# Four groups by seven products in each feed-forward stage, woven with ordinary steps, and silu as one ScalarE activation

## The chip, the cores and the metric

One core of a Trainium2 chip runs the whole kernel in one launch. The metric is the device time of one execution in microseconds (us). Engines are named as in the profile: PE is TensorE's matmul side and PEld its weight loads, DVE is VectorE, ACT is ScalarE, POOL is GpSimd, SP is SyncE, which issues nearly all loads.

## The reference, cut to what matters

The kernel computes one decoder block over 256 positions and a model width of 2048, in fp32:

```
h = x + 1/2 * SwiGLU_1(RMSNorm(h))          # feed-forward stage 1, inner width 5632 = 44 blocks of 128
h = h + W_out(mixer(RMSNorm(h) @ W_in))     # gated recurrence (8 heads) beside a short convolution
h = h + 1/2 * SwiGLU_2(RMSNorm(h))          # feed-forward stage 2, the same shape as stage 1
h = h + sigmoid(RMSNorm(h) @ W_pg) * (p @ W_pe)
y = RMSNorm_final(h)

swiglu(x) = (silu(x @ w_gate) * (x @ w_up)) @ w_down
```

The change touches the two feed-forward stages, the loop that emits all steps, and the sizes of some buffers that the mixer shares.

## The kernel before, in words

**Numbers in two parts.** Every fp32 weight block and every activation is split into a high part (a copy rounded to fp32r, made by ACT) and a low part (the rest, a subtraction by DVE). A product of two numbers is three matmuls: high by high, high by low, low by high. An ordinary step holds a 128-column block of weights (raw, 128 x 16 x 128 values): `load` (L100 ff.) issues its DMA on SP, `split` makes `hi` (L97, ACT) and `lo` (L98, DVE) in two halves of 128x1024, `product` (L116 ff.) runs for each of 16 k-blocks a 512-column matmul of `hi` (L120, both parts of the activation side by side) and a 256-column matmul of `lo` (L119 or L122). The epilogue adds the two halves of the PSUM bank (`halves`: ACT copy L146, DVE add L147) and scales it (L153).

**Feed-forward stage.** The inner width is cut into four chunks (`CHUNKS`: 8, 12, 12 and 12 blocks). For each chunk gate and up steps fill `hid`, then 16 down steps (each `nk` = 8 or 12 k-blocks) add into the residual `hT` (`partial`, L204 ff.: ACT L206, DVE L207 and L208). A gate epilogue is scaled, a Sigmoid (L158), and a DVE multiply (L375); an up epilogue multiplies with the gate (L381) and splits into `hid` (L162, L163).

**Groups by seven products.** In each of the last three chunks, four of the twelve blocks (4 gate and 4 up blocks together) are computed as a 2x2 block product with seven products in place of eight (Winograd's form): the tokens are two halves of 128, the k-blocks come in 8 pairs, and gate and up weights are 512 wide. `seven` (L273 ff.) makes 16 half steps out of a group: for each pair `kp` a half step "a" (3 products, 9 matmuls of 512 columns, lines L293 to L295) and a half step "b" (4 products, 12 matmuls). Seven PSUM banks of the eight hold the seven sums for the whole group, so one bank is left for the ordinary steps between. The combinations of the activations are made once per stage (`forms`, L253 ff.), written to DRAM by POOL's queue (L271) and read back with each pair (`xf`, L304). The weight combinations are made for each pair by DVE (`sp_a`, L320 to L322), and they are split like other weights (`pieces`, L309 ACT, L310 DVE). The group's raw weights have one buffer (`sraw`, `bufs=1`), loaded by L302. At the end `epi` (L335 ff.) adds the seven sums and applies silu (Sigmoid L343, two DVE multiplies L344, L345), and `turn` transposes the result into `hid` (L392, 8 transposes a group).

**Order.** The order is written out by hand. Each chunk with a group runs: two half steps, then ordinary gate or up step and half step in turn (14 of each), the last two ordinary steps, `turn`, then 16 down steps without any half steps. The main loop emits for step i: the load of step i + 3, the split of step i + 2, the matmuls of step i, its epilogue, its hooks. Hooks carry the extra work, such as `rows` at the stage's step 5 and `forms(kp)` at steps 6 + kp. From this the framework's scheduler makes one list of instructions per engine, which may differ from the order of the code where the inputs allow.

Of the kernel before, what the change touches and what calls it, by code (L numbers as in the profile page):

```python
# [14 lines left out]
P = 128  # L15
# [16 lines left out]

CHUNKS = ((8, 0), (12, 4), (12, 4), (12, 4))
NS = 4
NK2 = NB // 2

RAW_BUFS = 3
LOAD_AHEAD = 3
SPLIT_AHEAD = 2


class Step:


    def __init__(self, src, nk, mm, epi=None):
        self.src, self.nk, self.mm, self.epi = src, nk, mm, epi
        self.hooks = []
        self.before = self.after = self.ld = self.sp = None


@with_exitstack
def kernel(
# [87 lines left out]
    def new_ps():  # L140
        return psum.tile([P, T2], F32, tag="ps", name="ps")
# [84 lines left out]
    def add(*a, **k):  # L226
        steps.append(Step(*a, **k))
        return len(steps) - 1
# [12 lines left out]

    FA, FB = ("P1", "P2", "P6"), ("P5", "P3", "P7", "P4")
    FORMS = {"P4": 0, "P5": 1, "P6": 2, "P7": 3, "P3": 4}

# [8 lines left out]
    def forms(kp, c_gain, sd):  # L253
        pool = st["spool"]
        a = pool.tile([P, 5, P], F32, tag="ec", name="fa", bufs=2)
        f = pool.tile([P, 5, P], F32, tag="ey", name="ff", bufs=2)
# [5 lines left out]
        a11, a21, a12 = a[:, 0, :], a[:, 1, :], a[:, 2, :]  # L262
        V.tensor_tensor(a21, a21, rho, ALU.mult)
        V.tensor_tensor(f[:, 0, :], a[:, 3, :], rho, ALU.mult)
        V.tensor_tensor(f[:, 1, :], a21, f[:, 0, :], ALU.subtract)
        V.tensor_tensor(f[:, 2, :], f[:, 1, :], a11, ALU.subtract)
        V.tensor_tensor(f[:, 3, :], a11, a21, ALU.subtract)
        V.tensor_tensor(f[:, 4, :], a12, f[:, 2, :], ALU.add)
        A.activation(x[:, 0], f, AF.Copy)
        V.tensor_tensor(x[:, 1], f, x[:, 0].bitcast(F32), ALU.subtract)  # L270
        nc.gpsimd.dma_start(sd[:, kp, :], x.rearrange("p a f t -> p (a f t)").bitcast(F32))  # L271

    def seven(ws, sd, finish):  # L273
# [24 lines left out]
        def ld(kp):  # L298
            def f(s):
                pool = st["spool"]  # L300
                r = g["raw", kp] = pool.tile([P, 4, T2], F32, tag="sraw", name="sraw", bufs=1)
                nc.sync.dma_start(r, ws[kp])  # L302
                x = g["xf", kp] = pool.tile([P, 10 * P], F32, tag="xf", name="xf", bufs=2)
                nc.sync.dma_start(x, sd[:, kp, :])  # L304
            return f

        def pieces(hi, lo, todo):
            for sl, src in todo:
                A.activation(hi[:, sl, :], src, AF.Copy)  # L309
                V.tensor_tensor(lo[:, sl, :], src, hi[:, sl, :].bitcast(F32), ALU.subtract)  # L310

        def sp_a(kp):
            def f(s):
                pool, r = st["spool"], g["raw", kp]
                t = g["t", kp] = pool.tile([P, 3, T2], F32, tag="st", name="st", bufs=1)
                hi, lo = g["a", kp] = tuple(pool.tile([P, 3, T2], F32R, tag="a" + n, name="a" + n, bufs=1)
                                            for n in ("hi", "lo"))
                pieces(hi, lo, [(slice(0, 2), r[:, 0:2, :])])
# [3 lines left out]
                V.tensor_tensor(r[:, 3, :], t[:, 2, :], r[:, 1, :], ALU.add)  # L322
                pieces(hi, lo, [(2, t[:, 2, :])])
            return f

        def sp_b(kp):
            def f(s):
                pool, r, t = st["spool"], g["raw", kp], g["t", kp]
                hi, lo = g["b", kp] = tuple(pool.tile([P, 4, T2], F32R, tag="b" + n, name="b" + n, bufs=1)
                                            for n in ("hi", "lo"))  # L330

                pieces(hi, lo, [(slice(0, 3, 2), t[:, 0:2, :]), (slice(1, 4, 2), r[:, 2:4, :])])
            return f

        def epi(s):  # L335
            pool = st["spool"]

            def e(tag, bufs=2):
                return pool.tile([P, 5 * P], F32, tag=tag, name=tag, bufs=bufs)[:, :T2]
# [7 lines left out]
            a, c0, v = e("ea", 1), e("ec"), e("ey")  # L347
            A.activation(a, g["P1"], AF.Copy)
# [5 lines left out]
            V.tensor_tensor(a, g["P7"], a, ALU.add)  # L354
            c1 = e("ec")
            V.tensor_tensor(c1, g["P4"], a, ALU.add)
# [4 lines left out]
        for kp in range(NK2):  # L361
            for key, names, sp in (("a", FA, sp_a), ("b", FB, sp_b)):
                s = Step(None, 0, mm(kp, names, key), epi if key == "b" and kp == NK2 - 1 else None)
                s.sp = sp(kp)
                s.ld = ld(kp) if key == "a" else None
                res.append(s)
        return res

    def ffn(wg, wu, wsd, wd, c_gain, c_next, name):
# [15 lines left out]
        def turn(k0, c):  # L385

            for k in range(0, NS, 2):
                ps = new_ps()
                for i in range(2):
                    for w in range(2):  # L390
                        o = i * T + w * P
                        TE.transpose(ps[:, o:o + P], c[w][:, (k + i) * P:(k + i + 1) * P], ident)  # L392
                d = st["hid"][:, k0 + k:k0 + k + 2, :]
                p = ps.rearrange("p (k t) -> p k t", k=2)
                A.activation(d[:, :, :T], p, AF.Copy)
                V.tensor_tensor(d[:, :, T:], p, d[:, :, :T].bitcast(F32), ALU.subtract)

        i0 = len(steps)
        f0 = ng = 0
        for ci, (nf, ns) in enumerate(CHUNKS):  # L400
            last = ci == len(CHUNKS) - 1
            std = []
            for k in range(ns, nf):
                std.append(Step(wg[f0 + k], NB, *gemm_in(g_epi)))
                std.append(Step(wu[f0 + k], NB, *gemm_in(u_epi(k))))
            if ns:
                got = []
                h = seven(wsd[ng], sd, lambda *c, got=got: got.extend(c))
                ng += 1
                seq, std = [*h[:2]], std  # L410
                for x in h[2:]:
                    seq += [std.pop(0), x]
                seq += std
                seq[-1].hooks.append(lambda got=got: turn(0, got))
                steps.extend(seq)
            else:
                steps.extend(std)
            order = [*range(ns, nf), *range(ns)]
            for j in range(NB):
# [11 lines left out]
                add(wd[j][:, f0:f0 + nf, :], nf, mm, epi)  # L431
            f0 += nf
        at(i0 + 5, rows)
        for kp in range(NK2):
            at(i0 + 6 + kp, lambda kp=kp: forms(kp, c_gain, sd))

# [13 lines left out]
    def mixer():  # L450
# [590 lines left out]
```

## Time and profile before

| | us |
|---|---|
| median of 3 runs | 2029.08 (2026.64 to 2030.02) |
| the profiled execution, its own time | 2028.77 |
| its span, first to last instruction | 2027.0 |
| PE busy | 2002.1 (99%) |
| DVE busy | 1636.0 (81%) |
| ACT busy | 1117.1 (55%) |
| DMA, mean | 207 GB/s |

The span is what the trace covers; 1.8 us of the execution lie around it. Matmuls are pipelined, so a row's duration is longer than its share of PE: the distance from one start to the next is what a matmul costs. An engine that is off the critical path can be busy for 80% and still set when a buffer comes free.

### The profile page before, as it was taken

The numbers are of one execution on the slowest core, as the hardware profiler recorded it, in microseconds if no ns is written. First come the engines' busy times: TensorE is split into PE (matmuls) and PEld (weight loads), VectorE is DVE, ScalarE is ACT, GpSimd is POOL, SyncE is SP. The second block draws the span as 40 slices with busy tenths as digits, with TensorE's granted clock in tenths as the row PEclk, the third lists the DMA queues.
The fourth block names the chain that finished last, engine by engine and source line by source line (L and its number), as shares of the span: only waits on it lengthen the run. The fifth ranks groups of instructions, "written<-read, shape, count | busy, mean of one in ns | idle before, by whom it ended". The sixth has DMA issues, their size and how long they took to land.

```text
span 2027.0 us, 28859 instructions
## 1 busy us (share of the span) xinstructions
PE 2002.1 (99%) x11094; PEld 1731.7 (85%) x11094; DVE 1636.0 (81%) x2645; ACT 1117.1 (55%) x1716; POOL 11.6 (1%) x23
## 2 busy tenths in 40 slices
PE   8999999999999999999999999999999999999997
PEld 7888888888888888888888888888888888888886
DVE  8988886888688775689798789788968886887886
ACT  7655555555555554553566556455555555555663
POOL 0000000000000000000000000000000000000000
PEclk9999999999999999999999999999999999999998
DMA  8686666665665465544355567766666666654742
GB/s 293 211 277 242 233 205 216 219 237 200 222 232 198 156 212 187 189 166 146 129 184 187 187 227 274 226 232 226 208 208 224 232 202 220 228 202 153 249 164 84
DMA packets 69546, 419.93 MB, mean 207 GB/s; under 512 B 7712, under 2 KB 7968, under 8 KB 35744
## 3 DMA queue, kind: packets, MB, share of 16 engines
q1 hardware_dynamic: 67104, 407.60, 59.0%
q0 software_dynamic: 2304, 10.49, 1.3%
q8 instruction: 87, 1.43, 0.3%
q14 instruction: 51, 0.42, 0.1%
HBM read 405.48 MB, written 12.58 MB: 206 GB/s over the span
## 4 chain that ended last, share of the span: by engine, by line
PE 89%; DVE 4%; DMA 4%; issue 1%; ACT 1%; SPq 0%; DVEq 0%; ACTq 0%
PE ps L120 49%; PE ps L119 23%; PE ps L294 3%; PE ps L295 3%; PE ps L293 3%; PE ps L122 2%; DVE lo L98 2%; DMA sraw<-w1s 1%; DMA raw<-w1d 1%; DMA raw<-w1u 1%; PE ps L591 1%; PE ps L494 1%; PE ps L493 1%; PE ps L492 1%; DMA sraw<-w2s 1%
## 5 line engine op out<-in xcount | busy, mean ns | idle before, releaser
L120 PE MATMUL ps<-xs,hi 128*128 128x512 f32 x3056 | 1082.8, 395 | 9.5 <-DVE xs L167 6.1
L98 DVE TENSOR_TENSOR lo<-raw,hi 128x1024 fp32r<-128x1024 f32 (+2 forms) x660 | 751.1, 1139 | 239.3 <-ACT hi L97 235.7
L97 ACT ACTIVATE hi<-raw 128x1024 fp32r<-128x1024 f32 (+2 forms) x660 | 652.7, 990 | 516.6 <-PE ps L120 323.6
L119 PE MATMUL ps<-xs,lo 128*128 128x256 f32 x2865 | 801.5, 280 | 0.4 <-DVE lo L98 0.2
L120 PEld LDWEIGHTS ps<-xs,hi 128*128 128x128 f32 x3056 | 569.7, 188 | 137.5 <-ACT hi L97 7.2
L119 PEld LDWEIGHTS ps<-xs,lo 128*128 128x128 f32 x2865 | 538.0, 188 | 10.4 <-DVE lo L98 1.8
L120 PE MATMUL ps<-hid,hi 128*128 128x512 f32 x1384 | 477.6, 394 | 0.0
L119 PE MATMUL ps<-hid,lo 128*128 128x256 f32 x1258 | 354.4, 283 | 0.5 <-ACT hid L162 0.5
L120 PEld LDWEIGHTS ps<-hid,hi 128*128 128x128 f32 x1384 | 251.5, 188 | 48.8
L119 PEld LDWEIGHTS ps<-hid,lo 128*128 128x128 f32 x1258 | 236.2, 188 | 7.3 <-ACT hid L162 1.3
L309 ACT ACTIVATE ahi<-sraw 128x1024 fp32r<-128x1024 f32 x48 | 51.0, 1063 | 125.2 <-DMA sraw<-w1s 61.5
L146 ACT ACTIVATE t<-ps 128x256 f32<-128x256 f32 x191 | 70.2, 372 | 88.3 <-PE ps L120 88.3
L320 DVE TENSOR_TENSOR st<-sraw 128x1024 f32<-128x1024 f32 x48 | 58.8, 1224 | 69.2 <-DMA sraw<-w1s 38.7
L147 DVE TENSOR_TENSOR t<-ps,t 128x256 f32<-128x256 f32 x191 | 80.3, 421 | 24.0 <-ACT t L146 23.9
L120 PE MATMUL ps<-mixout,hi 128*128 128x512 f32 x240 | 83.6, 397 | 0.0
L153 DVE TENSOR_TENSOR t<-t,rb 128x256 f32<-128x256 f32 x183 | 76.9, 422 | 2.7
L293 PE MATMUL ps<-bhi,xf 128*128 128x512 f32 x192 | 74.9, 390 | 0.0
L295 PE MATMUL ps<-blo,xf 128*128 128x512 f32 x192 | 74.9, 390 | 0.0
L294 PE MATMUL ps<-bhi,xf 128*128 128x512 f32 x192 | 74.9, 390 | 0.0
L208 DVE SCALAR_TENSOR_TENSOR hT<-ps,t 128x256 f32<-128x256 f32 x141 | 59.7, 424 | 13.7 <-DVE t L207 1.4
L207 DVE TENSOR_TENSOR t<-hT,t 128x256 f32<-128x256 f32 x141 | 59.1, 420 | 10.6 <-ACT t L206 10.6
L206 ACT ACTIVATE t<-ps 128x256 f32<-128x256 f32 x141 | 51.9, 369 | 27.5 <-PE ps L120 27.5
(234 smaller groups left out, 2078.7 us busy)
## 6 DMA issues: line engine op xcount, KB each, us to landing
raw<-w_in SPq DMA_DIRECT2D x48, 1024.0 KB, 4.8
raw<-w1d SPq DMA_DIRECT2D x48, 768.0 KB, 4.2
raw<-w2d SPq DMA_DIRECT2D x48, 768.0 KB, 4.3
raw<-w2g SPq DMA_DIRECT2D x32, 1024.0 KB, 4.9
raw<-w2u SPq DMA_DIRECT2D x32, 1024.0 KB, 5.1
raw<-w1u SPq DMA_DIRECT2D x31, 1024.0 KB, 5.3
raw<-w1g SPq DMA_DIRECT2D x30, 1024.0 KB, 5.0
xf<-forms SPq DMA_DIRECT2D x48, 640.0 KB, 4.0
```

Of the source, the lines that this page charges most:

```text
L97: A.activation(hi[:, sl, :], r, AF.Copy)
L98: V.tensor_tensor(lo[:, sl, :], r, hi[:, sl, :].bitcast(F32), ALU.subtract)
L119: TE.matmul(ps[:, T:], lo, m[:, :T], start=False, stop=False)
L120: TE.matmul(ps, hi, m, start=first, stop=last)
L146: A.activation(t, ps[:, T:], AF.Copy)
L147: V.tensor_tensor(t, ps[:, :T], t, ALU.add)
L153: V.tensor_tensor(dst, t, rb, ALU.mult)
L207: V.tensor_tensor(t, hT[:, j, :], t, ALU.add)
L208: V.scalar_tensor_tensor(hT[:, j, :], ps[:, :T], c, t, ALU.mult, ALU.add)
L293: TE.matmul(g[p], x_lo, hi[:, i, :], start=kp == 0, stop=False)
L294: TE.matmul(g[p], x_hi, hi[:, i, :], start=False, stop=False)
L295: TE.matmul(g[p], x_hi, lo[:, i, :], start=False, stop=kp == NK2 - 1)
```

## The change

It does five things, in both feed-forward stages.

1. A fourth group replaces 4 more gate and 4 more up blocks. The chunks now have 0, 1, 1 and 2 groups.
2. `weave` spreads the half steps: group 1 among the gate and up steps of chunk 2, group 2 among the down steps of chunk 2, group 3 among the gate and up steps of chunk 3, group 4 among the down steps of chunk 3. `turn` becomes two steps of its own per group.
3. Silu is one ACT activation; the DVE multiplies L375 and L344 go.
4. The group's raw weights share the ring of raw buffers, now 4 deep (it was 3, and one for the groups). Loads are issued 4 steps ahead, splits up to 3 steps ahead with two rules that stop them. The combinations use one more form and one fewer special case, and the split of a half step's weights is one instruction per engine, 128x1536 or 128x2048.
5. `forms` runs at every second step, and some temporary buffers shrink (`t` 6 to 4, `s` 3 to 2, `nr` 4 to 3).

```diff
-CHUNKS = ((8, 0), (12, 4), (12, 4), (12, 4))
+CHUNKS = ((8, 0), (12, 1), (12, 1), (12, 2))
-RAW_BUFS = 3
-LOAD_AHEAD = 3
-SPLIT_AHEAD = 2
+RAW_BUFS = 4
+LOAD_AHEAD = 4
+SPLIT_AHEAD = 3
...
-    def tt(shape=(P, T), dtype=F32, tag="t", bufs=6):
+    def tt(shape=(P, T), dtype=F32, tag="t", bufs=4):
...
-        s = tt(tag="s", bufs=3)
+        s = tt(tag="s", bufs=2)
...
-        A.activation(x[:, 0], f, AF.Copy)
-        V.tensor_tensor(x[:, 1], f, x[:, 0].bitcast(F32), ALU.subtract)
+        A.activation(x[:, 0, 4, :], a22, AF.Copy)
+        A.activation(x[:, 0, :4, :], f, AF.Copy)
+        V.tensor_tensor(x[:, 1, 4, :], a22, x[:, 0, 4, :].bitcast(F32), ALU.subtract)
+        V.tensor_tensor(x[:, 1, :4, :], f, x[:, 0, :4, :].bitcast(F32), ALU.subtract)
...
-                r = g["raw", kp] = pool.tile([P, 4, T2], F32, tag="sraw", name="sraw", bufs=1)
+                r = wpool.tile([P, NB, P], F32, tag="raw", name="raw", bufs=RAW_BUFS)
+                r = g["raw", kp] = r.rearrange("p (a b) c -> p a (b c)", a=4)
...
+        def parts(key, kp, n, src):
+            hi, lo = g[key, kp] = tuple(st["spool"].tile([P, n, T2], F32R, tag=key + t, name=key + t, bufs=1)
+                                        for t in ("hi", "lo"))
+            A.activation(hi, src, AF.Copy)
+            V.tensor_tensor(lo, src, hi.bitcast(F32), ALU.subtract)
...
-                y = e("ey")
-                A.activation(y, c, AF.Sigmoid, scale=rt[:, 0:1])
-                V.scalar_tensor_tensor(c, c, rt[:, 0:1], y, ALU.mult, ALU.mult)
-                V.scalar_tensor_tensor(c, u, rt[:, 0:1], c, ALU.mult, ALU.mult)
+                y = e("ey", 2)
+                A.activation(y, c, AF.Silu, scale=rt[:, 0:1])
+                V.scalar_tensor_tensor(c, u, rt[:, 0:1], y, ALU.mult, ALU.mult)
...
+        (c0, d0), (c1, d1), (c2, d2), (c3, d3) = others
+        g1, g2, g3, g4 = groups
+        def alternate(x, h):
+            seq = [*h[:2]]
+            for i in range(2, 16):
+                seq += [x[i], h[i]]
+            return seq
+        steps.extend([*c0, *d0])
+        first = alternate([None, None, *c1[:14]], g1[0])
+        steps.extend([*first, *c1[14:], *g1[1]])
+        steps.extend([*d1[:2], *alternate(d1, g2[0])])
+        steps.extend([*c2[:2], *g2[1], *alternate(c2, g3[0])])
+        steps.extend([*d2[:2], *alternate(d2, g4[0])])
+        steps.extend([*c3[:2], *g3[1], *c3[2:4], *g4[1], *c3[4:], *d3])
...
-            s = sig(g)
-            V.tensor_tensor(g, g, s, ALU.mult)
+            A.activation(g, g, AF.Silu)
...
-            at(i0 + 6 + kp, lambda kp=kp: forms(kp, c_gain, sd))
+            at(i0 + 6 + 2 * kp, lambda kp=kp: forms(kp, c_gain, sd))
...
-            d = m["m1"].tile([P, T], F32R, tag="nr", name="nr", bufs=4)
+            d = m["m1"].tile([P, T], F32R, tag="nr", name="nr", bufs=3)
...
+    loaded = done = 4
     for i, s in enumerate(steps):
-        if 0 < i < n - LOAD_AHEAD:
-            load(steps[i + LOAD_AHEAD])
-        if 1 < i < n - SPLIT_AHEAD:
-            split(steps[i + SPLIT_AHEAD])
+        while i > 0 and loaded < min(n, i + LOAD_AHEAD + 1):
+            load(steps[loaded])
+            loaded += 1
+        while 1 < i and done < min(n, i + SPLIT_AHEAD + 1):
+            x = steps[done]
+            if x.kind == "w" and sum(y.kind == "w" for y in steps[i:done]) > 2:
+                break
+            if x.kind in ("a", "b") and any(y.kind == x.kind for y in steps[i:done]):
+                break
+            split(x)
+            done += 1
```

In `weave`, `c0` to `c3` are the gate and up steps of the chunks, `d0` to `d3` their down steps; `g[0]` is the 16 half steps of a group and `g[1]` its two `turn` steps.

## Rows read from the trace of the kernel before

**Rows 1.** The page: the span, and busy time of each engine.

```profile
span 2027.0 us, 28859 instructions
...
PE 2002.1 (99%) x11094; PEld 1731.7 (85%) x11094; DVE 1636.0 (81%) x2645; ACT 1117.1 (55%) x1716; POOL 11.6 (1%) x23
```

**Rows 2.** Timeline of PE, 199.5 to 218 us: start us, us, then the instruction.

```profile
199.80 0.40 PE L293 MATMUL ps<-bhi,xf 128*128 128x512 f32 x1
...
202.53 0.40 PE L120 MATMUL ps<-xs,hi 128*128 128x512 f32 x1
...
208.15 0.39 PE L293 MATMUL ps<-ahi,xs 128*128 128x512 f32 x1
...
210.23 0.40 PE L120 MATMUL ps<-xs,hi 128*128 128x512 f32 x1
```

**Rows 3.** Timeline of PE: first group's transposes, first down step, second group's start.

```profile
277.96 1.04 PE L392 MATMUL ps<-cst,ec 128*128 128x128 f32 x8
278.75 0.48 PE L120 MATMUL ps<-hid,hi 128*128 128x512 f32 x1
...
346.34 0.39 PE L293 MATMUL ps<-ahi,xs 128*128 128x512 f32 x1
```

**Rows 4.** Windows over six group stretches: length, engines' busy (count), PEclk, DMA share, GB/s.

```profile
148.98:278.75 129.77, 129.59 (x689) 110.44 (x688) 113.01 (x153) 73.68 (x100) 0.00 (x0) 1.00 0.66 227
346.34:476.65 130.31, 129.95 (x690) 110.37 (x688) 111.50 (x150) 73.38 (x99) 0.00 (x0) 1.00 0.65 226
544.24:673.58 129.34, 129.34 (x689) 110.45 (x688) 107.13 (x144) 70.14 (x95) 0.00 (x0) 1.00 0.60 209
1316.96:1446.15 129.19, 129.19 (x689) 110.63 (x688) 111.62 (x150) 73.93 (x99) 0.00 (x0) 1.00 0.64 224
1513.74:1644.39 130.65, 129.50 (x689) 110.55 (x688) 111.82 (x150) 73.68 (x99) 0.00 (x0) 1.00 0.64 225
1711.98:1841.51 129.53, 129.53 (x689) 110.47 (x688) 107.49 (x144) 70.37 (x95) 0.00 (x0) 1.00 0.59 209
```

**Rows 5.** Timelines of SP, DVE and PE around 1580 us; in brackets idle before.

```profile
1571.89 0.33 SPq L302 DMA_DIRECT2D sraw<-w2s  x1
...
1579.53 1.23 DVE L320 TENSOR_TENSOR st<-sraw 128x1024 f32<-128x1024 f32 x1 [4.08 <-DMA sraw<-w2s]
...
1584.06 0.51 PE L120 MATMUL ps<-xs,hi 128*128 128x512 f32 x1 [1.15 <-DVE t L147]
```

**Rows 6.** First chunk of stage 1: PE's two idle times, and the windows row.

```profile
60.03 0.50 PE L120 MATMUL ps<-xs,hi 128*128 128x512 f32 x1 [0.96 <-ACT hi L97]
...
70.13 0.39 PE L122 MATMUL ps<-xs,lo 128*128 128x256 f32 x1 [1.16 <-DVE lo L98]
...
45.00:103.00 58.00, 55.88 (x318) 48.10 (x317) 56.93 (x141) 39.12 (x69) 3.87 (x7) 1.00 0.60 207
```

**Rows 7.** Groups by line of DVE, shapes apart: busy, mean ns, idle before.

```profile
L98 DVE TENSOR_TENSOR lo<-raw,hi 128x1024 fp32r<-128x1024 f32 x460 | 562.2, 1223 | 144.6 <-ACT hi L97 141.4
L98 DVE TENSOR_TENSOR lo<-raw,hi 128x768 fp32r<-128x768 f32 x192 | 183.4, 957 | 93.9 <-ACT hi L97 93.5
...
L321 DVE TENSOR_TENSOR st<-st,sraw 128x512 f32<-128x512 f32 x48 | 32.9, 685 | 0.0
```

**Rows 8.** Timeline of DVE, three instructions with no idle time between them.

```profile
204.06 0.42 DVE L163 TENSOR_TENSOR hid<-t,hid 128x256 fp32r<-128x256 f32 x1
204.40 1.22 DVE L310 TENSOR_TENSOR blo<-st,bhi 128x1024 fp32r<-128x1024 f32 x1
205.53 1.22 DVE L310 TENSOR_TENSOR blo<-sraw,bhi 128x1024 fp32r<-128x1024 f32 x1
```

**Rows 9.** Groups by line: what frees a down step's PSUM bank.

```profile
L208 DVE SCALAR_TENSOR_TENSOR hT<-ps,t 128x256 f32<-128x256 f32 x141 | 59.7, 424 | 13.7 <-DVE t L207 1.4
...
L206 ACT ACTIVATE t<-ps 128x256 f32<-128x256 f32 x141 | 51.9, 369 | 27.5 <-PE ps L120 27.5
```

**Rows 10.** Timeline of ACT: the table load ahead of the first Sigmoid.

```profile
51.88 1.28 ACT L158 ACT_TABLE_LOAD   x1
```

More of the change, by code (lines that the diff above doesn't have):

```diff
@@ L48, in __init__ @@
         self.before = self.after = self.ld = self.sp = None
+        self.kind = "w"
 @with_exitstack
@@ L312, in sp_a @@
         def sp_a(kp):
             def f(s):
[L314 to L318, printed above, removed]
+                r = g["raw", kp]
+                parts("a", kp, 3, r[:, 0:3, :])
@@ L326, in sp_b, with e @@
         def sp_b(kp):
[L327 to L333, printed above, removed]
+            return lambda s: parts("b", kp, 4, g["t", kp])
         def epi(s):
             pool = st["spool"]
-            def e(tag, bufs=2):
-                return pool.tile([P, 5 * P], F32, tag=tag, name=tag, bufs=bufs)[:, :T2]
+            def e(tag, bufs):
+                return pool.tile([P, T2], F32, tag=tag, name=tag, bufs=bufs)
@@ L348, in epi @@
+            a, c0, v = e("ea", 1), e("ec", 4), e("ey", 2)
             A.activation(a, g["P1"], AF.Copy)
@@ L364, in seven @@
                 s.sp = sp(kp)
+                s.kind = key
                 s.ld = ld(kp) if key == "a" else None
@@ L367, in seven, with weave @@
         return res
+    def weave(groups, others):
+        (c0, d0), (c1, d1), (c2, d2), (c3, d3) = others
[12 more added lines that the diff above has]
+        steps.extend([*c3[:2], *g3[1], *c3[2:4], *g4[1], *c3[4:], *d3])
     def ffn(wg, wu, wsd, wd, c_gain, c_next, name):
@@ L385, in turn, with step, mm, epi @@
         def turn(k0, c):
[L387 to L396, printed above, removed]
+            def step(k):
+                def mm(s):
+                    s.ps = new_ps()
+                    for i in range(2):
+                        for w in range(2):
+                            o = i * T + w * P
+                            TE.transpose(s.ps[:, o:o + P], c[w][:, (k + i) * P:(k + i + 1) * P], ident)
+                def epi(s):
+                    d = st["hid"][:, k0 + k:k0 + k + 2, :]
+                    p = s.ps.rearrange("p (k t) -> p k t", k=2)
+                    A.activation(d[:, :, :T], p, AF.Copy)
+                    V.tensor_tensor(d[:, :, T:], p, d[:, :, :T].bitcast(F32), ALU.subtract)
+                s = Step(None, 0, mm, epi)
+                s.sp = lambda s: None
+                s.kind = None
+                return s
@@ L398, in ffn @@
+            return [step(k) for k in range(0, NS, 2)]
         i0 = len(steps)
-        f0 = ng = 0
-        for ci, (nf, ns) in enumerate(CHUNKS):
+        groups = []
+        others = []
+        f0 = 0
+        for ci, (nf, ng) in enumerate(CHUNKS):
             last = ci == len(CHUNKS) - 1
-            std = []
-            for k in range(ns, nf):
+            for i in range(ng):
+                got = []
+                h = seven(wsd[len(groups)], sd, lambda *c, got=got: got.extend(c))
+                groups.append((h, turn(i * NS, got)))
+            std, down = [], []
+            for k in range(ng * NS, nf):
@@ L404, in ffn @@
                 std.append(Step(wg[f0 + k], NB, *gemm_in(g_epi)))
                 std.append(Step(wu[f0 + k], NB, *gemm_in(u_epi(k))))
[L406 to L417, printed above, removed]
@@ L418, in ffn @@
-            order = [*range(ns, nf), *range(ns)]
+            order = [*range(ng * NS, nf), *range(ng * NS)]
             for j in range(NB):
@@ L430, in epi @@
                         partial(s.ps, j, 0.5)
-                add(wd[j][:, f0:f0 + nf, :], nf, mm, epi)
+                down.append(Step(wd[j][:, f0:f0 + nf, :], nf, mm, epi))
+            others.append((std, down))
             f0 += nf
+        weave(groups, others)
         at(i0 + 5, rows)
         for kp in range(NK2):
-            at(i0 + 6 + kp, lambda kp=kp: forms(kp, c_gain, sd))
+            at(i0 + 6 + 2 * kp, lambda kp=kp: forms(kp, c_gain, sd))
         def open_hid(s):
@@ L1007, in sevens @@
         res, f0 = [], 0
-        for nf, ns in CHUNKS:
-            if ns:
-                g, u = (w[:, f0 * P:(f0 + NS) * P].reshape(NK2, 2, P, NS * P) for w in (gate, up))
+        for nf, ng in CHUNKS:
+            for i in range(ng):
+                c = slice((f0 + i * NS) * P, (f0 + (i + 1) * NS) * P)
+                g, u = (w[:, c].reshape(NK2, 2, P, NS * P) for w in (gate, up))
                 res.append(np.stack([g[:, 0], g[:, 1], u[:, 1], u[:, 0]], 2))
```

35 lines of the change are left out of this document (14 added, 21 removed).

## Prediction

> **What bounds the kernel now.** I read the page first. PE is busy for 2002.1 of 2027.0 us, DVE for 81% of the span [rows 1]. So PE is the bound, and only two things can make the kernel faster: fewer matmul columns, or less of the 25 us in which PE idles. The execution took 2028.77 us, 0.31 below the median of 2029.08; I apply the sum to the median.
>
> PE's timeline gives the price of each kind of step as a distance between starts. In a group stretch a half step b lasts 202.53 - 199.80 = 2.73 us, an ordinary gate or up step 208.15 - 202.53 = 5.62, a half step a 210.23 - 208.15 = 2.08 [rows 2]. The 8 transposes of a group take 278.75 - 277.96 = 0.79, and 16 down steps of 12 blocks (346.34 - 278.75) / 16 = 4.22 each [rows 3].
>
> The six stretches from a group's first half step to the end of its transposes hold 16 ordinary steps, 8 a, 8 b and the transposes: 16 x 5.62 + 8 x (2.08 + 2.73) + 0.79 = 129.19 us with no wait at all. They took 129.19 to 130.65, 3.65 us more in sum [rows 4]. So PE hardly waits there, though DVE is busy for 83 to 87% of them. The largest wait shows the mechanism: the group's raw weights have one buffer, their load was issued at 1571.89, DVE stood 4.08 us until it landed at 1579.5, and the bank of the ordinary step before was then emptied late, so PE idled 1.15 us at 1584.06 [rows 5]. PE also idles 0.96 and 1.16 us in the first chunk of stage 1, where DVE is busy for 56.93 of 58 us [rows 6]. There `forms` runs at eight steps in a row.
>
> **The change, part by part.**
>
> *A fourth group.* It takes 8 ordinary steps away, 8 x 5.62 = 44.96 us, and adds 8 x (2.08 + 2.73) + 0.79 = 39.27 [rows 2, 3]. That is 5.69 less per stage, 11.4 for both, all of it on PE and so on the path. A 512-column matmul costs (208.15 - 202.53) x 2/3 / 16 = 0.234 us here by its share of columns, at a granted clock of 1.00, that is 2.4 GHz [rows 2, 4]. The Trainium skill (TensorE: Matmul & The Clock Gate, section "Wait — 56ns, not 53.3ns?") gives start to start the columns over 2.4 GHz plus about 2.5 ns, which is 0.216. The trace does not agree, and the measurement decides; by the page the saving would be an estimated 9 us.
>
> *Silu as one activation.* 28 gate steps per stage and each group's two halves lose a DVE multiply. DVE's work comes by distance between starts: 0.34 us for 256 columns, 1.13 for 1024 [rows 8]. The rows' own means are some 0.09 longer, 1.223 for 1024 [rows 7], so I take 685 - 90 = 0.60 for 512 and 957 - 90 = 0.87 for 768, and on the same line 1.67 for 1536 and 2.2 for 2048. PE gains nothing directly. Silu may belong to another table than Sigmoid, which mixer and last stage keep: then three more loads of 1.28 us each stand on ACT [rows 10], at mixer, stage 2 and last stage. I cost them at nothing, because ACT is busy for 55% [rows 1] and PE has finished splits for two steps ahead; without that cover they cost up to 3.8. The Trainium skill (ScalarE: Activation LUTs, section "Table sets: the hidden batching unit") speaks against mixing functions of two sets; with its drain it prices a switch at 2.66 us, an estimated 8 us on ACT. No run here shows which set holds Silu.
>
> *Forms at every second step.* The same DVE work, five of the eight in the first chunk and three among the first down steps. DVE in the window of 58 us loses three forms of about 2.0 us (six instructions of 128 columns and one of 640 on the same line) and seven multiplies of 0.34: about 48 of 58. I expect both idles of rows 6 to go: -2.1. The three moved ones find down steps of 8 blocks; PE has slack in finished splits there. POOL's stores move with them, and its queue holds nothing else.
>
> *One ring of raw buffers, loads 4 ahead.* The wait of rows 5 came from the one buffer. In the new ring a load waits for the split of four loads before, several steps ahead of use. SP's queue also carries the reads of the forms, which wait for half steps long past. Each group reads 8 x 1.64 MB in place of 8 MB of blocks; among down steps two steps and a pair move 3.2 MB in 13.25 us, 241 GB/s, against 227 at a DMA share of 0.66 now [rows 4]. I cost it at nothing and take the 3.65 us away: -3.7. If the loads did queue, the rest of rows 5 would stay.
>
> *DVE in the new stretches.* Among gate and up steps a pair of half steps and two ordinary steps need 1.67 + 1.13 + 2 x 0.60 + 2.2 = 6.2 for the pair, 4 x 1.13 + 6 x 0.34 = 6.56 for the two. With 9 + 2 instructions of 0.60 at the end a stretch needs 8 x 12.76 + 6.6 = 109 of 129 us, 84%. Among down steps it is 8 x (6.2 + 4 x 0.87 + 4 x 0.34) + 6.6 = 95 of 107 us, 89%. So DVE stays below PE everywhere, but no light stretch is left between groups.
>
> *The joints.* At a group's end DVE owes the sums (5.4), the next two ordinary steps, and the first pair of the next group, which comes without a step between. From group 3 to 4: 5.4 + 4.84 + 6.2 = 16.4, less two splits done ahead (3.5), against 2 x 4.22 + 2.08 = 10.5 of PE: 2.4 late. From 2 to 3: 5.4 + 6.56 + 1.2 + 6.2 - 4.5 = 14.9 against 14.1: 0.8 late. From 1 to 2, with four ordinary steps between: not late. That is 3.2 per stage, 6.4 in all as the upper end, nothing as the lower, if the third step of look-ahead does its work in time. I take 4, nearer the upper end, because these prices come from rows of full DVE.
>
> *One free bank between down steps.* A group holds seven of the eight banks. A gate step's bank is free after ACT 0.37 and one DVE instruction; a down step's needs two, L207 and L208: 0.37 + 0.42 + 0.42 plus hand-over, about 1.5 us [rows 9]. It has 2.08 (a) or 2.73 (b). Slack is 0.6, and one long instruction of 2.2 us in the way uses it up. Lower end nothing, as in most stretches of rows 4; upper end half of 2.2 less 0.6, 0.5 us at each of 28 boundaries before an a half step: 14. I take 2, by the nearest row, since rows 4 show about 0.6 us per stretch under the same kind of wait.
>
> *Smaller buffers, the two `turn` steps, main loop.* The mixer's temporaries are read within a step or two of being written, four are enough: nothing, upper end 2.
>
> The sum: -11.4 - 2.1 - 3.7 + 4 + 2 = **-11.2**, so 2029.1 - 11.2 = **2017.9**.
>
> **The rivals.**
>
> *Everything covered (0.10).* Joints and banks cost nothing: -17.2, 2011.9. For it: the look-ahead grows, and DVE no longer stands on the group's load. Against it: 89% of DVE with no pause.
>
> *DVE falls behind (0.14).* Both ends above come together: -17.2 + 6.4 + half of 14 = -3.8, 2025; with the mixer's 2 and the loads 2029, no difference. For it: ACT-then-DVE chains in the sums stand while silu is computed. Against it: now 87% costs 0.6 us a stretch [rows 4].
>
> *The bank decides (0.07), slower.* In all 56 boundaries between down step and half step (28 per stage) the eviction stands behind a 1536- or 2048-wide split. Each loses s; all gains are gone from s = 17.2 / 56 = 0.31 us, and at 0.6 the time is 2029 - 17 + 34 = 2046. For it: rows 5, where exactly such a queue cost 1.15 us once. Against it: that happened after a wait for a load, which goes away.
>
> *Silu switches tables back and forth (0.03).* If Copy were not in Silu's table, 72 silus would bring 144 loads x 1.28 = 184 us onto ACT [rows 10]. ACT is at 73 of 130 us in a stretch [rows 4] and would go to about 95, in the chain of every gate step: 2030 to 2050. Against it: today Sigmoid and Copy alternate after one load.
>
> **How the numbers follow.** The forecast itself (0.66) holds 2013 to 2024. With the covered case at 0.10 and the better half of the third at 0.07 the range is 2010.5 to 2027; left out are the slower cases and the rest. Faster by over 0.2% means below 2025.0; 0.2% is about what a measurement of this kernel can tell from no change. Faster: 0.66 + 0.10 + 0.04 = 0.80. Within: 0.10, from the third case. Slower: 0.07 + 0.03 = 0.10.
>
> **What would show it.** Half steps of 2.08 and 2.73 us, 64 of each and half of them among down steps of 4.22; no DVE multiply after a gate's silu; no idle on L302's data; idle of PE at the first pair of groups 3 and 4, released by a split; table loads at the stage borders only. Wrong would be PE idle behind the down steps' L208 at every other step, DVE above 95% in the down stretches, or ACT loads within a chunk.

## The result and the profile after

The changed kernel takes **2053.89 us** (median of 4 runs, 2051.20 to 2056.08); the kernel before took 2028.96 beside it. The ratio is 1.0121, interval [1.0108, 1.0133]: slower by 1.2%, and outside the predicted range.

The page of the kernel after, span and busy times:

```profile
span 2054.3 us, 28494 instructions
...
PE 2007.3 (98%) x10934; PEld 1719.0 (84%) x10934; DVE 1659.6 (81%) x2495; ACT 1127.1 (55%) x1617; POOL 11.6 (1%) x23
```

Against [rows 1] 160 matmuls and 150 DVE instructions are gone, as planned, yet the span is 27.3 us longer and PE's busy share fell. Each norm starts with one matmul on PE that sums squares (`row_scale`, L190 before, L191 after), so windows between the starts of that matmul are the stages. First stage, mixer and second stage of the kernel before (length, then PE, PEld, DVE, ACT, POOL busy, PEclk, DMA share, GB/s):

```profile
37.29:747.59 710.30, 706.43 (x3870) 607.83 (x3868) 585.23 (x902) 394.26 (x587) 7.14 (x11) 1.00 0.65 219
747.59:1186.93 439.34, 439.14 (x2492) 384.27 (x2493) 338.73 (x611) 229.15 (x360) 0.00 (x0) 1.00 0.51 175
1186.93:1915.24 728.31, 726.88 (x4003) 627.76 (x4002) 599.60 (x911) 404.09 (x596) 4.26 (x8) 1.00 0.64 219
```

The same of the kernel after:

```profile
37.85:758.03 720.18, 706.98 (x3788) 600.58 (x3786) 598.52 (x827) 397.78 (x532) 7.12 (x11) 1.00 0.64 223
758.03:1200.42 442.39, 440.48 (x2495) 384.72 (x2494) 339.38 (x610) 232.12 (x363) 0.00 (x0) 1.00 0.50 173
1200.42:1942.91 742.49, 730.67 (x3923) 621.75 (x3922) 609.15 (x836) 406.14 (x544) 4.25 (x8) 1.00 0.64 223
```

The feed-forward stages lost 9.88 and 14.18 us, the mixer 3.05. Within a stage the two groups that run among gate and up steps are clean: from the first half step to the last they take 117.3 to 118.9 us, and 8 pairs with 14 ordinary steps between are 8 x (2.08 + 2.73) + 14 x 5.62 = 117.2 [rows 2]. The two among down steps should take 38.48 + 14 x 4.22 = 97.6 [rows 2, 3]. They took 103.6, 106.7, 106.3 and 104.9: 31 us over in sum, for the four of both stages. Windows over these four, transposes and neighbouring down steps included:

```profile
278.92:391.21 112.29, 108.64 (x556) 89.72 (x554) 93.60 (x109) 61.52 (x70) 0.00 (x0) 1.00 0.68 240
521.00:636.15 115.15, 109.35 (x554) 89.45 (x553) 93.89 (x111) 59.89 (x68) 0.00 (x0) 1.00 0.63 223
1461.40:1576.34 114.94, 109.93 (x556) 90.98 (x553) 93.62 (x109) 61.43 (x70) 0.00 (x0) 0.99 0.67 235
1706.10:1819.47 113.37, 108.90 (x553) 89.45 (x552) 93.77 (x111) 60.00 (x68) 0.00 (x0) 1.00 0.65 226
```

DVE is busy for 93.6 to 93.9 us, some 83% of them: no engine is full, and all of them wait. For what, the groups by line say (PE, fourth stretch: busy, mean ns, then idle before and its releaser):

```profile
L121 PE MATMUL ps<-hid,hi 128*128 128x512 f32 x192 | 68.8, 397 | 3.1 <-DVE hT L209 3.0
L295 PE MATMUL ps<-bhi,xf 128*128 128x512 f32 x32 | 12.7, 398 | 0.9 <-ACT bhi L312 0.9
L297 PE MATMUL ps<-blo,xf 128*128 128x512 f32 x33 | 11.4, 404 | 0.5 <-DVE blo L313 0.4
```

L209 is the last of the three instructions that empty a down step's PSUM bank (ACT L207, then DVE L208 and L209; L206 to L208 in the kernel before, [rows 9]). The view of that one line shows who waited for it in the whole run (us, times):

```profile
L209 DVE SCALAR_TENSOR_TENSOR hT<-ps,t x141: 410/424/426, 108.8 to 1937.2; 128x256 f32<-128x256 f32 x141
...
  PE ps L121: 11.0, 15
```

In the four stretches PE's idle sums to 18.8 us: 11.1 behind L209, 7.8 behind the half steps' splits. The rest of the 31 us is matmuls that start further apart, around such waits and in the 3.4 us of halved clock described at the end. PE's list also lost its alternation there: up to three down steps follow each other, then several half steps. The worst single wait for a bank stands between two such down steps, once in each stretch:

```profile
364.90 0.48 PE L121 MATMUL ps<-hid,hi 128*128 128x512 f32 x1 [1.55 <-DVE hT L209]
```

Most of the other waits show one picture on DVE. The list puts a split of a later down step's weights (L99, 0.95 us) between L208 and L209, and often a 2048-wide split in front of both (here PE waits 0.43 us, until 348.92):

```profile
344.94 2.29 DVE L313 TENSOR_TENSOR blo<-st,bhi 128x2048 fp32r<-128x2048 f32 x1 [0.93 <-ACT bhi L312]
347.15 0.42 DVE L208 TENSOR_TENSOR t<-hT,t 128x256 f32<-128x256 f32 x1
347.48 0.95 DVE L99 TENSOR_TENSOR lo<-raw,hi 128x768 fp32r<-128x768 f32 x1
348.35 0.42 DVE L209 SCALAR_TENSOR_TENSOR hT<-ps,t 128x256 f32<-128x256 f32 x1
```

Counted over the 64 down steps of the four stretches, L99 stands between the two at 42, another instruction at 12, none at 10.

### The profile page after: what moved, and what is told of

It is laid out like the page before. It is cut to its first block, busy times and chain, and to the rows that moved or that the text cites. A ratio compares the mean times of both kernels' runs of the same rounds, so it can differ in the third digit from the quotient of the medians.

```text
span 2054.3 us, 28494 instructions
## 1 busy us (share of the span) xinstructions
PE 2007.3 (98%) x10934; PEld 1719.0 (84%) x10934; DVE 1659.6 (81%) x2495; ACT 1127.1 (55%) x1617; POOL 11.6 (1%) x23
## 4 chain that ended last, share of the span: by engine, by line
PE 84%; DVE 6%; ACT 4%; DMA 3%; issue 3%; SPq 0%; DVEq 0%; ACTq 0%
PE ps L121 45%; PE ps L120 21%; PE ps L297 4%; PE ps L295 4%; PE ps L296 4%; PE ps L123 2%; DMA raw<-w1s 1%; ACT hi L98 1%; ACT bhi L312 1%; DVE lo L99 1%; DVE blo L313 1%; PE ps L608 1%; DMA raw<-w2s 1%; DVE alo L313 1%; PE ps L509 1%
## 5 line engine op out<-in xcount | busy, mean ns | idle before, releaser
L121 PE MATMUL ps<-xs,hi 128*128 128x512 f32 x2800 | 989.9, 395 | 6.3 <-ACT hi L98 6.0
L99 DVE TENSOR_TENSOR lo<-raw,hi 128x1024 fp32r<-128x1024 f32 (+2 forms) x628 | 709.9, 1133 | 230.4 <-ACT hi L98 228.2
L120 PE MATMUL ps<-xs,lo 128*128 128x256 f32 x2625 | 734.9, 280 | 0.0
L121 PEld LDWEIGHTS ps<-xs,hi 128*128 128x128 f32 x2800 | 521.7, 188 | 119.5 <-ACT hi L98 6.0
L121 PE MATMUL ps<-hid,hi 128*128 128x512 f32 x1384 | 491.9, 398 | 11.1 <-DVE hT L209 11.0
L120 PEld LDWEIGHTS ps<-xs,lo 128*128 128x128 f32 x2625 | 493.1, 188 | 8.6 <-DVE lo L99 0.6
L313 DVE TENSOR_TENSOR blo<-st,bhi 128x2048 fp32r<-128x2048 f32 x64 | 146.7, 2292 | 68.3 <-ACT bhi L312 62.9
L312 ACT ACTIVATE bhi<-st 128x2048 fp32r<-128x2048 f32 x64 | 122.6, 1915 | 51.5 <-DVE st L322 40.6
L312 ACT ACTIVATE ahi<-raw 128x1536 fp32r<-128x1536 f32 x64 | 95.2, 1488 | 48.4 <-DMA raw<-w1s 16.0
L313 DVE TENSOR_TENSOR alo<-raw,ahi 128x1536 fp32r<-128x1536 f32 x64 | 112.1, 1752 | 4.7 <-ACT ahi L312 4.3
L295 PE MATMUL ps<-bhi,xf 128*128 128x512 f32 x256 | 100.8, 394 | 2.9 <-ACT bhi L312 2.9
L296 PE MATMUL ps<-bhi,xf 128*128 128x512 f32 x256 | 100.0, 391 | 0.0
L297 PE MATMUL ps<-blo,xf 128*128 128x512 f32 x256 | 95.8, 399 | 3.0 <-DVE blo L313 2.8
L207 ACT ACTIVATE t<-ps 128x256 f32<-128x256 f32 x141 | 52.7, 374 | 57.1 <-PE ps L121 57.0
L320 DVE TENSOR_TENSOR st<-raw 128x1024 f32<-128x1024 f32 x64 | 78.0, 1219 | 5.1 <-DMA raw<-w1s 2.7
```

What stands on the lines that cost most here:

```text
L99: V.tensor_tensor(lo[:, sl, :], r, hi[:, sl, :].bitcast(F32), ALU.subtract)
L120: TE.matmul(ps[:, T:], lo, m[:, :T], start=False, stop=False)
L121: TE.matmul(ps, hi, m, start=first, stop=last)
L295: TE.matmul(g[p], x_lo, hi[:, i, :], start=kp == 0, stop=False)
L296: TE.matmul(g[p], x_hi, hi[:, i, :], start=False, stop=False)
L297: TE.matmul(g[p], x_hi, lo[:, i, :], start=False, stop=kp == NK2 - 1)
```

## The experiments

Each is the changed kernel with one edit, unless said otherwise. Theory A: the down stretches lose because a down step's bank is freed too late; within it, the order of instructions on DVE (G) or the length of the chain (C). Rivals: the reads of the forms in SP's queue; PE's disordered list (O); silu; the rest of the change.

**Three groups.** The group among down steps is left out of each stage; the rest of the change stays.

```diff
-CHUNKS = ((8, 0), (12, 1), (12, 1), (12, 2))
+CHUNKS = ((8, 0), (12, 1), (12, 1), (12, 1))
...
+        for d, c, g, e in ((d1, c2, g2, d2), (d2, c3, g3, d3)):
+            steps.extend([*d, *alternate([None, None, *c[:14]], g[0]), *c[14:], *g[1]])
```

> The changed kernel with three groups per stage in place of four, all three among gate and up steps, none among down steps; silu, the ring of raw buffers, the merged splits, the spread forms and the smaller buffers stay. Theory A (the loss is made where half steps stand among down steps, 31.7 us of PE waits in the four such stretches of the changed kernel): the time falls to 2053.9 - 31.7 + 11.4 (a group's saving given back in each stage) = 2034, with 1 us or less of PE idle in each group stretch. Theory B (the ring, the wide splits or the smaller buffers cost wherever a group runs): at or above 2045, with waits at half steps among gate and up steps.

Measured: 2030.0 us, ratio 0.9999 [0.9990, 1.0009]. The loss is in the down stretches. The other parts (forms, ring, silu, buffers) are worth nothing net, but that is a difference of two terms. Its first stage, mixer and second stage:

```profile
38.64:745.88 707.24, 704.75 (x3869) 607.70 (x3868) 571.56 (x816) 391.51 (x544) 7.14 (x11) 1.00 0.63 221
745.88:1189.56 443.68, 441.75 (x2494) 385.68 (x2493) 339.35 (x610) 231.72 (x363) 0.00 (x0) 1.00 0.50 171
1189.56:1916.72 727.16, 726.40 (x4003) 627.39 (x4002) 582.60 (x825) 400.52 (x555) 4.26 (x8) 1.00 0.64 221
```

Against the kernel before, the stages are 3.06 and 1.15 us shorter, 4.21 together, and the mixer is 4.34 longer.

**The bank's reader first.** The two DVE instructions of `partial` are swapped, so that the one that reads PSUM comes first (it is then L208) and no longer waits for the other's sum.

```diff
-        V.tensor_tensor(t, hT[:, j, :], t, ALU.add)
-        V.scalar_tensor_tensor(hT[:, j, :], ps[:, :T], c, t, ALU.mult, ALU.add)
+        V.scalar_tensor_tensor(hT[:, j, :], ps[:, :T], c, hT[:, j, :], ALU.mult, ALU.add)
+        V.tensor_tensor(hT[:, j, :], hT[:, j, :], t, ALU.add)
```

> The changed kernel with the two DVE instructions of a down step's epilogue swapped, so that the one that reads the PSUM bank comes first and no longer waits for ACT's copy and the other instruction: the bank is free about 0.4 to 0.8 us earlier. Theory A1 (the eviction of the one free bank decides; PE waits for the second DVE instruction add up to 11.1 us in the four down stretches): 6 to 11 us faster than the changed kernel, 2043 to 2048. Theory A2 (the eviction is late only because DVE and ACT stand on late splits and loads ahead of it in their queues): within 3 us of 2053.9.

Measured: 2022.19 us, 0.9964 [0.9951, 0.9977], faster than both kernels. Its windows: first stage, mixer, second stage, and the first and last down stretch:

```profile
38.56:742.96 704.40, 700.26 (x3788) 601.13 (x3787) 596.81 (x827) 398.96 (x532) 7.13 (x11) 1.00 0.65 228
742.96:1185.33 442.37, 440.46 (x2496) 384.57 (x2495) 339.40 (x610) 232.16 (x363) 0.00 (x0) 1.00 0.51 173
1185.33:1908.13 722.80, 721.68 (x3924) 621.02 (x3923) 607.68 (x835) 407.55 (x543) 4.26 (x8) 1.00 0.66 229
...
288.00:385.60 97.60, 97.60 (x506) 83.21 (x505) 86.63 (x100) 55.87 (x61) 0.00 (x0) 1.00 0.74 255
...
1688.80:1786.50 97.70, 97.70 (x505) 83.09 (x504) 84.36 (x98) 54.01 (x60) 0.00 (x0) 1.00 0.72 248
```

PE is busy for every one of the 97.60 us. Swapping two instructions of 0.42 us gave 15.78 + 19.69 = 35.47 us in the two stages, several times what I expected of it; the late splits and most of the list's disorder went with the bank's waits. 30.9 of it lie in the four down stretches, which went from 421.5 us to 390.6; the rest lies elsewhere, where waits of 1 to 2 us and falls of the clock differ from run to run. So theory A holds, with a price that I still had too small.

**Splits in pieces.** The half steps' wide ACT and DVE instructions (1536 and 2048 columns) are cut into 1024 and 512 again.

```diff
-            A.activation(hi, src, AF.Copy)
-            V.tensor_tensor(lo, src, hi.bitcast(F32), ALU.subtract)
+            for i in range(0, n, 2):
+                sl = slice(i, min(n, i + 2))
+                A.activation(hi[:, sl, :], src[:, sl, :], AF.Copy)
+                V.tensor_tensor(lo[:, sl, :], src[:, sl, :], hi[:, sl, :].bitcast(F32), ALU.subtract)
```

> The changed kernel with the half steps' weight splits in pieces of 1024 and 512 columns again, in place of 1536 and 2048. Theory A3 (a wide split of 1.75 or 2.29 us stands in front of short evictions, and a half step waits for all of its weights at once): 5 to 15 us faster than the changed kernel, 2039 to 2049, with fewer waits at the first matmul of a half step. Theory A2 (late loads and order of the queues): the pieces only cost DVE some 0.1 us each, 2052 to 2058.

Measured: 2026.16 us, 0.9985 [0.9976, 0.9995], better than I expected; down stretches 98.4 to 98.9 us, and PE waits for L209 nowhere. The same bank with the same three instructions is free in time when the instructions in front of them are short, though at some 40 of the 64 down steps another still stands between L208 and L209.

**The reads of the forms on POOL's queue.**

```diff
-                nc.sync.dma_start(x, sd[:, kp, :])
+                nc.gpsimd.dma_start(x, sd[:, kp, :])
```

> The changed kernel with the reads of the forms issued by POOL in place of SP, so that on SP no weight load stands behind a read that waits for PE to finish a half step. Theory A2a (raw weights land late because SP stood on those reads, 19.8 us in the first down stretch, and ACT then stands on the load): 8 to 20 us faster than the changed kernel, 2034 to 2046, and the waits of ACT on the groups' raw weights shrink. Rival (loads are late because their buffers are freed late by the splits): within 3 us of 2053.9.

Measured: 2073.78 us, 1.0217 [1.0201, 1.0233]. Moving the reads did not help, but it does not clear SP's queue by itself: PE's waits for L209 fell from 11.0 to 5.2 us, and new ones came at the split ahead of the half steps (21.6 us before L295 on `ahi`, from L312). Why that split comes later was not followed further. What clears the queue is the swap above: the reads stay on SP there, and PE waits for nothing in the stretches.

**PE in the code's order.** PE's list, only, is held to the code's order in the four down stretches, where each half step follows a down step.

```diff
...
+            region.enter_context(tc.manual_schedule(engines={mybir.EngineType.PE}))
```

> The changed kernel, every instruction the same, with PE's list held in the order of the code in the two down stretches with a group of each stage (down step, half step, down step, half step); the lists of the other engines stay the scheduler's. Theory O (the loss is made by PE's list: in the changed kernel's trace half steps stand side by side and two or three down steps follow each other there, although the code alternates them): the four stretches shrink from 104.9 to 106.7 us to 97 to 99 from the first half step to the last, 24 to 31 us in all, and the time is 2022 to 2030. Theory A1 (a down step's eviction and the splits are too slow for any order): waits of 0.5 us or more stay at most down steps, 2045 or more.

Measured: 2059.0 us, 1.0143 [1.0124, 1.0162]; stretches 103.3, 108.1, 103.3 and 107.0, the loss unchanged. So O falls: putting the list in order took nothing off, and the waits came at other places. With the order regular, the mechanism can be read off the timeline. DVE and PE of this kernel (its L298, L314, L321 are L297, L313, L320 of the others):

```profile
326.75 0.42 DVE L208 TENSOR_TENSOR t<-hT,t 128x256 f32<-128x256 f32 x1
327.08 1.22 DVE L321 TENSOR_TENSOR st<-raw 128x1024 f32<-128x1024 f32 x1
328.22 0.41 DVE L209 SCALAR_TENSOR_TENSOR hT<-ps,t 128x256 f32<-128x256 f32 x1
```

```profile
327.77 0.39 PE L298 MATMUL ps<-alo,xf 128*128 128x512 f32 x1
328.78 0.47 PE L121 MATMUL ps<-hid,hi 128*128 128x512 f32 x1 [0.62 <-DVE hT L209]
```

The down step ended at 326.1, L207 on ACT took until 326.5, L208 until 327.2. Then DVE's list has a sum of raw weights of 1.22 us, for a later half step, ahead of L209. The half step of 2.08 us is over, all eight banks are taken, PE waits 0.62. How often PE waits so in this run, by the view of L209 (us, times; at 18 of the 26 the sum of 1.22 us stands between L208 and L209, at the others L99):

```profile
  PE ps L121: 20.8, 26
```

**PE and DVE in the code's order.** As the last run, with DVE's list held too. No operation changes; L209 then stands right behind L208.

```diff
-engines={mybir.EngineType.PE}
+engines={mybir.EngineType.PE, mybir.EngineType.DVE}
```

> PE and DVE both keep the code's order in the four down stretches (the run before it held PE alone: 2059.0 us, stretches 103.3 to 108.1, and there one 1024-wide DVE instruction of 1.13 us stood between L208 and L209 at most down steps). In the code's order L209 stands directly behind L208, with the same operations. Theory G (the bank is late because a long DVE instruction gets between L208 and L209): the steady wait of 0.62 us behind L209 goes, the stretches fall to 98 to 100 us, the time to 2025 to 2033. Rival C (the chain of three instructions itself, ACT and then two on DVE, is too long for a half step): the wait stays, stretches 103 to 108, time 2050 to 2065. If the order of the code makes DVE wait for ACT elsewhere, the waits carry another name than L209.

Measured: 2039.54 us, 1.0046 [1.0030, 1.0062]; stretches 100.5, 100.4, 102.0, 101.9. The steady wait is gone:

```profile
  PE ps L121: 10.3, 4
```

So G holds and C falls: the chain of three fits a half step if nothing stands in it. The time is above what I expected because one wait of 2.54 to 2.59 us per stretch is left, at the first pair, where a 2048-wide split stands in front of L208; in the last two stretches the clock fell behind it:

```profile
297.95 2.29 DVE L314 TENSOR_TENSOR blo<-st,bhi 128x2048 fp32r<-128x2048 f32 x1 [0.84 <-ACT bhi L313]
300.16 0.42 DVE L208 TENSOR_TENSOR t<-hT,t 128x256 f32<-128x256 f32 x1
300.69 0.42 DVE L209 SCALAR_TENSOR_TENSOR hT<-ps,t 128x256 f32<-128x256 f32 x1
```

**Two and two.** PE in order, but two down steps and then two half steps, so that two down steps meet.

```diff
+        def pairs(x, h):
+            seq = [*h[:2]]
+            for i in range(2, 16, 2):
+                seq += [*x[i:i + 2], *h[i:i + 2]]
+            return seq
...
```

> The changed kernel with PE's list held in order in the down stretches, but that order now has two down steps, then two half steps, in turn: seven places per stretch where a down step follows a down step while a group holds seven banks. Theory O (such a place costs what it costs in the changed kernel, 1.55 us, until the one bank is empty): 7 x 4 x 1.55 = 43 us more than with the alternating order, 2060 to 2072. Rival (the order of steps does not matter, only how early splits are ready): within 8 us of the run with the alternating order.

Measured: 2160.98 us, 1.0653 [1.0628, 1.0678]; stretches 129.8 to 133.7. Its line on L209, and the first stretch with 7 us out of it:

```profile
  PE ps L121: 82.8, 28
```

```profile
287.10:420.80 133.70, 113.15 (x505) 94.73 (x504) 88.90 (x101) 55.07 (x60) 0.00 (x0) 0.87 0.54 187
298.50:305.50 7.00, 5.09 (x16) 4.44 (x17) 5.14 (x8) 0.00 (x0) 0.00 (x0) 0.54 0.39 131
```

28 boundaries cost 2.96 us of idle each, nearly twice the 1.55 that I had expected, and the granted clock fell again and again.

**Two and two, the bank's reader first.** The last two edits together.

> As the run with two down steps in a row, with the epilogue's two DVE instructions swapped so that the bank's reader does not wait for the other. Theory O with the bank as the cause of the price: the wait at each of the 28 places falls from about 1.55 us to 0.7 to 0.9, so 17 to 24 us faster than that run, 2038 to 2050. If the price at such a place is a late split or load instead, the swap gives less than 5 us.

Measured: 2080.84 us, 1.0253 [1.0238, 1.0268], 80 us less than without the swap, where I expected about 20, and still well above the 2050 that I named. Here L208 reads the bank, and PE still waits for it at all 28 places, 1.51 us each (us, times; then the first stretch, to set beside the row above):

```profile
  PE ps L121: 42.2, 28
```

```profile
289.20:399.90 110.70, 100.78 (x505) 84.34 (x504) 88.58 (x101) 55.09 (x60) 0.00 (x0) 0.98 0.65 226
```

So the swap halves the wait and does not end it. The idle fell by 40.6 us, half of the 80; the rest is the clock, 0.87 over the first stretch without the swap and 0.98 with it.

**Silu alone, on the kernel before.**

```diff
-            s = sig(g)
-            V.tensor_tensor(g, g, s, ALU.mult)
+            A.activation(g, g, AF.Silu)
```

(and the same in `silu_mul`).

> The kernel before with silu as one activation and nothing else of the change. My term for this edit was nothing: five table loads in place of two, none of them followed by an idle PE, 2027 to 2031 us, ratio 0.999 to 1.001. Rival 1 (the lighter DVE lets PE lose less in the group stretches): those lose up to the 3.65 us that they had over their ideal, 2025.5. Rival 2 (three table loads of 1.28 us on the path at the stage borders): up to 4 us more, 2033.

Measured: 2028.84 us, 0.9998 [0.9987, 1.0009]. Nothing, as the prediction's term had it.

**The bank's reader first, on the kernel before.** The swap of the second experiment.

> The kernel before with the down step's bank read first (the two DVE instructions of the epilogue swapped), nothing else. Theory A (the late bank costs only where a half step stands between two down steps): before has none, so no difference, 2027 to 2031 us. Rival (reading the bank first helps every down step, also in stretches of down steps alone): each of the two stages loses several us, below 2024.

Measured: 2029.48 us, 0.9998 [0.9989, 1.0007]. In this kernel no group runs among down steps, so these have all eight banks, and the order of the eviction is free. It has a price where a group holds seven banks and a half step stands between two uses of the eighth. Which of the two it takes, few banks or a short step, this run does not part.

**Versions that beat both.** The swap with a fourth buffer for the mixer's norm rows (and one sigmoid temporary less):

```diff
-tag="nr", name="nr", bufs=3
+tag="nr", name="nr", bufs=4
-        s = tt(tag="s", bufs=2)
+        s = tt(tag="s", bufs=1)
```

> The changed kernel with the swapped epilogue (2022.2 us in its run) and the mixer's row buffers at four again; room comes from the Sigmoid's temporary, one in place of two. Theory M (3 us of the changed kernel's loss are in the mixer, where ACT waits with a row buffer until PE has read another and PE then idles 1.6 us at 1043 us): the wait goes, 2018 to 2020. Rival (the mixer is longer for another reason, the ring or the shorter list of temporaries): 2021 to 2024; slower still if the one Sigmoid temporary makes ACT wait.

Measured: 2021.76 us, 0.9959 [0.9944, 0.9973]. And that with the splits in pieces too:

> The changed kernel with the bank read first, the half steps' splits in pieces of 1024 and 512 again, and four buffers for the mixer's norm rows (one buffer less of the sigmoid temporaries to make room). Theory: the down stretches stand at 97.6 with the bank alone, so pieces add little there; what they take away is the wait of 1.00 us on a 2048-wide split at a group's first pair, once or twice a stage: 2018 to 2021. Rival: more instructions on ACT and DVE give it back, 2022 to 2024. The 1.6 us wait for the norm rows in the mixer (there with three buffers and with four) stays.

Measured: 2023.09 us, 0.9963 [0.9951, 0.9976]. These two and the swap alone can't be told apart. The mixer's wait of 1.6 us for the norm rows stays with four buffers as with three.

## Why the prediction was wrong

**The step that failed** is "One free bank between down steps": "I take 2, by the nearest row". The term was about 31 us and not 2: the swap alone gives 35.47 us back in the two stages, 30.9 of it in the four down stretches. This splits the loss, and does not test it: -11.41 against the kernel before, +35.47 for the bank and +3.05 for the mixer are the differences of the windows, and add up to 27.1 of the 27.3 us between the two spans. Three things went wrong in that one term.

- *The nearest row was not near.* I took the 0.6 us per stretch of [rows 4]. There a half step follows an ordinary gate or up step, and that step's bank is free after ACT and one DVE instruction. A down step's chain goes from ACT to DVE and through two instructions of a list into which the scheduler puts others.
- *Slack of 0.6 us was held against a rare event.* The words "one long instruction of 2.2 us in the way uses it up" reckon with a single wide instruction. Much less is enough, and it is the usual case: in the changed kernel an instruction stands inside the chain, between L208 and L209, at 54 of 64 down steps, by 0.95 us mostly, and with PE in order by 1.22 at 18 of 26 waits.
- *The upper end of 14 counted the wait alone.* Late banks made splits late (7.8 us of idle), and each wait also widened the distances between matmuls. The swap took all of it away together. How much of the 35.47 us each link carries was not measured. The prediction's own sign of being wrong, PE idle behind the eviction (L208 there, L209 now), did come, but only 15 times and for 11.0 us, so that sign alone would have shown a third of the price.

**The rival that came true** in kind is "the bank decides", with a chance of 0.07: 56 boundaries, 0.6 us each, 2046. Measured, 35.47 / 56 = 0.63 per boundary, or 30.9 / 56 = 0.55 by the down stretches alone; its time was short by the gains of forms and ring that it also counted, and the mixer. What I held against it, that rows 5 showed the queue only behind a late load, was no argument: the load made DVE late there, a full list makes it late here. Its turning point of 0.31 us a boundary was twice the real one, (11.41 - 3.05) / 56 = 0.15, because of the gains that did not come.

**The other steps.**

- *PE is the bound, and a fourth group saves 11.4.* Right in kind: with the bank out of the way the stages lose 5.90 and 5.51 against the kernel before, together 11.41. That this is the forecast figure is luck. The run with three groups had already lost 4.21 of it by the other parts of the change; from three groups to four with the swap the stages lose 2.84 and 4.36, so the fourth group is worth 7.2 where the prediction had 11.4. What takes the other 4 was not tried.
- *Forms (-2.1) and ring (-3.7).* The waits named did go: L302's data no longer hold DVE (69.2 us of idle before L320 in the kernel before, 5.1 after), and both idles of [rows 6] are gone. Of the 5.8 us forecast for the two, the stages of the run with three groups show at most 4.21, and the mixer takes as much back, so its ratio is 0.9999. The prediction's 241 GB/s for a down stretch was low: 1024 + 640 + 2 x 768 KB in 13.25 us are 247, and the run with the swap moved 248 to 255 there while PE waited for nothing. In `after` ACT stands 3.58 us on a forms buffer (`x`, two of them) that POOL's store has not left, and PE idles 2.16 some ten microseconds later:

```profile
95.24 0.31 ACT L269 ACTIVATE xf<-fa 128x128 fp32r<-128x128 f32 x1 [3.58 <-DMA forms<-xf]
```

```profile
105.61 0.39 PE L120 MATMUL ps<-hid,lo 128*128 128x256 f32 x1 [2.16 <-ACT hid L163]
```

  That the first wait causes the second is argued from their order, and was not tried.
- *Silu.* Right: DVE work falls, PE gains nothing, five table loads in place of two stand at the stage borders and cost PE nothing. The load at 46.30 stands close between two ACTIVATEs, 1.28 us with no drain beside it. So the 2.66 us, drain included, that the prediction quoted from the Trainium skill (ScalarE: Activation LUTs, section "What ACT_TABLE_LOAD costs") do not show at this load:

```profile
45.90 0.39 ACT L147 ACTIVATE t<-ps 128x256 f32<-128x256 f32 x1
46.30 1.28 ACT L388 ACT_TABLE_LOAD   x1
47.60 0.72 ACT L388 ACTIVATE t<-t 128x256 f32<-128x256 f32 x2
```

- *DVE's 95 us in a down stretch.* About right (93.6 to 93.9 in the windows above). But a busy share says what an engine does, and not how long one instruction waits in its list: with the swap DVE is busy for 86.63 of 97.60 us, the forecast 89%, and PE does not wait at all.
- *Joints, +4.* Too high: with the swap all four down stretches stand at 97.6 to 97.7 and their neighbours at 117.3 to 119.0; the look-ahead covers them. The 119.0 has a wait of 1.00 us for a split at the first pair of group 1 (at 163.15), where the prediction saw no delay.
- *Mixer buffers, 0, at most 2.* Measured 3.03 to 3.05, in the kernel with the swap too, and not in silu alone. 1.6 us of it is one wait of PE for a norm row:

```profile
1030.34 0.78 PE L679 MATMUL ps<-nr,ones_r 128*128 128x256 f32 x2 [1.60 <-ACT nr L673]
```

  The norm rows' buffers are not it, since four leave it as it was. ACT's list has them behind a split that waits 1.22 us for PE (at 1043.92 in the changed kernel). The temporaries `t`, cut from 6 buffers to 4, and the longer look-ahead of the splits were not put back, so the cause stays open. Where the clock fell behind that wait, the mixer is longer still (443.68 with three groups).

## What to carry to other kernels

Before shorter steps are put between others, hold the chain that frees the resource they share (here the one spare PSUM bank) against the shortest step, with the longest instruction of each engine's list in its way as the rule, not as the exception; a busy share of 83% does not rule out that wait. Let the instruction that reads the bank come first and do the sums on SBUF after it: that cost nothing here and gave 1.5%, and where no group held the other banks it changed nothing. A bound from a neighbouring row counts only if that row has the same chain of releasers.

## What the runs showed of the hardware

The granted clock fell to half, 1.2 GHz, for stretches of 3.4 us. In the kernel after, the first two falls stand right behind a wait of 2.16 us (to 105.61, above) and one of 2.35 us (to 1522.44); the windows rows have PEclk third from the end:

```profile
106.00:109.40 3.40, 3.40 (x12) 2.81 (x12) 1.57 (x5) 1.33 (x2) 0.00 (x0) 0.51 0.96 362
...
1522.50:1525.90 3.40, 3.40 (x10) 2.92 (x11) 3.37 (x3) 0.00 (x0) 0.00 (x0) 0.50 0.72 298
```

3.4 us at half speed lose another 1.7, so such a wait costs nearly twice itself (estimated from these rows). The third fall, at 1870.6, followed waits of only 0.49 and 0.61 us. After the mixer's 1.60 us the clock stayed up in the run with the swap and fell in the one with four norm-row buffers, so which short wait brings it down was not settled. With a late bank at every second boundary, as in the first run of two and two, it averaged 0.87 over a stretch, and that is the half of the swap's 80 us there that is not idle. In the kernel before it fell only at the very end.
